# Norm factors folded into the weights, low weight parts on VectorE: a hybrid GLA and neighbourhood-attention layer

## The chip, the core and the metric

The kernel runs on one core of a Trainium2 chip. The metric is the device time of one launch in microseconds (us). The engines are named as in the profile: PE is TensorE (PEld its weight loads), DVE is VectorE, ACT is ScalarE, POOL is GpSimd, SP is the engine whose queue issues most DMAs.

## The reference

One encoder layer on 1024 tokens and 16 meta tokens of width 1024. The steps that matter here:

```
u = x * rsqrt(mean(x*x, -1) + eps) * norm_g          # pre-norm, norm_g has one factor per model column
z = u @ w_in                                          # one projection, its columns split into:
gq, gk, gv, r_f, r_b, g_gate, nq, nk, nv, n_gate = split(z)
# group A: gated linear attention, 4 heads, chunks of 64 tokens, a forward and a backward scan
o_gla = rmsnorm(scan_f(gq, gk, gv, decay(r_f)) + scan_b(...)) * silu(g_gate)
# group B: neighbourhood attention, 16 heads of 64, 8 x 16 window plus 16 meta keys
q, k = rmsnorm(nq) * q_norm_g, rmsnorm(nk) * k_norm_g
o_na = softmax(q k / 8 + rpb + meta_bias) v * silu(n_gate)
out = x + concat(o_gla, o_na) @ w_out
```

The factors norm_g stand on the contracted axis of the projection, so `(x*g) @ w` and `x @ (g*w)` are the same product; the factor 1/rms of a token is applied behind the projection, on its output.

## The kernel before, in words

**Products.** Every fp32 product is made of three TensorE passes over a high and a low part of each operand (`mm3`, L409 to L413): high x high (L411), high x low and low x high (L412, L413). A high part is a rounded copy, a low part what the rounding left. The token operand is kept whole in `uh` (high) and `ul` (low), eight blocks k of 128 model columns by 1024 tokens. The weights pass by in 150 pieces of up to 128x512, each loaded by an SP DMA into one of five `raw` buffers and split by `piece_split` (L240 to L261) into one of nine pairs of buffers, `wh` and `wl`. The split of piece j is followed on SP's queue by the load of piece j+5, into the raw buffer that it frees. A piece is split when a pair of buffers is free: `release` lets the next one go. Pieces of the attention pairs hold one block k ("pack" 1, 128x512, the first pair's 128x384); the last gate's pieces hold four blocks of 128 columns, the GLA pieces two of 256, the first GLA value pieces one of 288.

**Who splits before.** For most pieces of the first part of the kernel (tables `SPLIT_ACT` and `NA1_ACT`) ACT makes the high part (L254) and POOL the low part (L255); for the others DVE does both (L257, L258). From the second GLA head on (`gpool` set) ACT and DVE share it (L251, L252).

**Order of the work.** A planner with a clock of its own (`S`) emits the instructions: `S.defer(ns, f)` emits f when its clock has advanced by ns, and each engine then runs its own list in the order of emission. The first 60 us are laid out by hand (`START_AT`: at which product, counted over the first pair's tiles, a token tile is loaded, split, squared, its 1/rms made and spread).

**Stages.** (1) The start: the first pair's eight natural tiles (`pn_na`, 128 tokens by 384 columns, eight blocks k) are computed while tokens arrive. Tiles 0 and 1 are computed side by side (`first_pair`), their token parts made block by block (`u_part`, L341 to L346); tiles 2 to 7 by halves of a tile (`u_split`, L348 to L358), each half first multiplied by g on DVE (L354). `u_rstd` squares the token rows on ACT, into a PSUM bank (`junk`, L365), and POOL raises the mean to the power -1/2 (L210). To have 1/rms on all partitions, with tokens along the free axis (`rbc`, used by gates, L484), `u_diag` (L373) multiplies the identity by the column of 1/rms on DVE, and `u_spread` (L378) multiplies it by a block of ones on PE. Constants of the attention (`na_static`, L491 to L530) are copied into the key and query buffers K2 and Q2 on DVE. (2) Eight attention pairs p: the natural tiles of pair p+1 and then its gate (`pz_na`, transposed) are the bulk of PE's work, and the attention steps u of pair p (scores, softmax, transposes `pp` of the probabilities P, product with v) are laid between. In a step, P is normalised on DVE for its two halves a (reciprocal L813, multiplication L815), PE transposes it (L826), and the result is copied to SBUF, for a=0 on ACT (L830), for a=1 on DVE (L832). A pair's last natural tile gives its eight pairs of weight buffers back, so the splits of the next eight pieces stand around each pair's end, beside the attention step 7. `k_prep` opens a pair's attention: PE transposes the keys (`kt`, L693) after DVE has normalised them (`nat`, L557). (3) The GLA heads, (4) the output projection. Between (2) and (3) the decay weights are loaded (`wdst`), cut (`wd`, L1018 to L1022), and the first gates `gt` evacuated (L484).

Of the kernel before, what the change touches and what calls it, by code (L numbers as in the profile page):

```python
# [19 lines left out]
NKB = 8  # L20
# [30 lines left out]

START_AT = {'load': {2: 9, 3: 15, 4: 18, 5: 21, 6: 27, 7: 34}, 'split': {2: 15, 3: 19, 4: 25, 5: 28, 6: 41, 7: 48}, 'rows': {0: 10, 1: 12, 2: 18, 3: 21, 4: 23, 5: 29, 6: 45, 7: 53}, 'rstd': {0: 15, 1: 16, 2: 21, 3: 27, 4: 35, 5: 43, 6: 48, 7: 55}, 'evac': {0: 18, 1: 21, 2: 27, 3: 35, 4: 43, 5: 52, 6: 59}, 'diag': {0: 31, 1: 42, 2: 42, 3: 55, 4: 55}, 'spread': {0: 46, 1: 63, 2: 57, 3: 59}}
BANKS = {2: ("po", 1), 3: ("pp", 2), 4: ("pp", 2), 5: ("pd", 2), 6: ("pd", 2), 7: ("po", 1)}
PUMP_AT = 5
LD_NS = (842.0, 589.0, 1838.0)
LS_NS = (376.0, 9817.0, 2715.0, 3855.0)
# [4 lines left out]
GZ_DVE = (1, 1, 0, 1)  # L61

SPLIT_ACT = {'na': (1, 1, 1, 0), 'gz': (1, 0, 1, 0), 'gv': (1, 1, 1, 0), 'gg': (1, 0, 1, 0)}
NA1_ACT = (1, 0, 1, 0, 1, 1, 1, 1)
SILU_STEP = 1
# [71 lines left out]
def kernel(  # L137
# [105 lines left out]
    def piece_split(j):  # L243
        if j < len(pieces):
# [4 lines left out]
            r = raw.pop(j)  # L249
            if gpool[0] is not None:  # L250
                act.activation(wh[:, :n], r[:, :n], AF.Copy)  # L251
                dve.tensor_tensor(wl[:, :n], r[:, :n], f32(wh[:, :n]), OP.subtract)  # L252
            elif (NA1_ACT[j - 8] if 8 <= j < 16 else SPLIT_ACT[key[0]][j % 4]):
                act.activation(wh[:, :n], r[:, :n], AF.Copy)  # L254
                pool.tensor_tensor(wl[:, :n], r[:, :n], f32(wh[:, :n]), OP.subtract)  # L255
            else:
                dve.tensor_copy(wh[:, :n], r[:, :n])  # L257
                dve.tensor_tensor(wl[:, :n], r[:, :n], f32(wh[:, :n]), OP.subtract)  # L258
            for t in range(pack):
# [80 lines left out]
    def u_part(b, k):  # L340

        xk = xs[b][:, k * 128 : k * 128 + 128]
        ts = slice(b * 128, b * 128 + 128)
        g = gT[:, k : k + 1]
        act.activation(uh[:, k, ts], xk, AF.Copy, scale=g)
        dve.scalar_tensor_tensor(ul[:, k, ts], xk, g, f32(uh[:, k, ts]), OP.mult, OP.subtract)  # L346

    def u_split(b):  # L348

        ts = slice(b * 128, b * 128 + 128)  # L350
        x3 = xs[b].rearrange("p (k t) -> p k t", k=NKB)
        halves = (slice(0, 4), slice(4, 8))
        for ks in halves:
            dve.tensor_tensor(x3[:, ks], x3[:, ks], gT[:, ks, None].to_broadcast([128, 4, 128]), OP.mult)  # L354
        for ks in halves:
            act.activation(uh[:, ks, ts], x3[:, ks], AF.Copy)  # L356
        for ks in halves:
            dve.tensor_tensor(ul[:, ks, ts], x3[:, ks], f32(uh[:, ks, ts]), OP.subtract)  # L358

    def u_rstd(b):  # L360

        st = nap.tile([128, 2], F32, tag="ust", name=f"ust{b}", bufs=2)
        for i in range(2):
            junk = ps_tile("ps", f"junk{b}_{i}", 2)
            act.activation(junk, xr[b][:, 512 * i : 512 * i + 512], AF.Square, accum_out=st[:, i : i + 1])  # L365
        dve.tensor_tensor(st[:, 0:1], st[:, 0:1], st[:, 1:2], OP.add)
        rstd(rs[:, b : b + 1], st[:, 0:1], 1.0 / 1024, 1)

    dg = {}

    def u_diag(b):
        dg[b] = nap.tile([128, 128], F32, tag="dg", name=f"dg{b}", bufs=3)
        dve.tensor_scalar(dg[b], ident, rs[:, b : b + 1], None, OP.mult)  # L373

    def u_spread(b):

        ps = ps_tile("ps", f"rb{b}", 2)
        pe.matmul(ps[:, 0:128], ones, dg[b], start=True, stop=True)  # L378
        act.activation(rbc[:, b * 128 : b * 128 + 128], ps[:, 0:128], AF.Copy)
        S.adv(220)  # L380

    def u_meta():
# [16 lines left out]
        def parts():  # L399
            xv3 = xm[:, 0:128].rearrange("p (k t) -> p k t", k=NKB)  # L400
            dve.tensor_tensor(xv3, xv3, gT[:, :, None].to_broadcast([128, NKB, 16]), OP.mult)
            dve.tensor_tensor(xv3, xv3, r[:, None, :].to_broadcast([128, NKB, 16]), OP.mult)
# [89 lines left out]
    def na_static(part):  # L492
        if part == 0:
# [5 lines left out]
            def copies():  # L499
                dve.tensor_copy(K2[0][64:128, :, 0:128], sv[64:128])  # L500
                dve.tensor_copy(K2[1][0:64, :, 0:128], sv[0:64])

        elif part == 1:
# [31 lines left out]
    def dense_na(p):  # L535
# [65 lines left out]
        for b in range(8):  # L601
# [882 lines left out]
```

## Time and profile before

| what | value |
|---|---|
| device time, three runs | 1160.01, 1161.38, 1161.72 us; median 1161.38 us |
| profiled execution | 1161.92 us, of which 1159.1 us are the span of the trace |
| granted TensorE clock, mean | 0.997 of full speed |
| busy share of the span | PE 97%, PEld 85%, DVE 67%, ACT 46%, POOL 26% |

An engine's busy time is summed over the span; a page of the profile tells which groups of instructions it consists of, the view of waits tells what an engine stood still for, and the timeline gives single instructions with their start and duration in us. Three stages follow each other: the start until about 63 us, the attention pairs until about 629 us, GLA and output projection until the end.

### The profile page before, as it was taken

Reading aid. Unit: us, or ns where it says so; the run is one execution under the profiler, and the core shown is the slowest. Engines: PE = TensorE matmul, PEld = TensorE weight load, DVE = VectorE, ACT = ScalarE, POOL = GpSimd, SP = SyncE. Lnnn points to the kernel's source line nnn. Section 1 sums busy time; section 2 is a strip of 40 time slices with the busy share of each in tenths; the row PEclk is TensorE's granted clock in tenths of the full one; section 3 lists DMA queues with packets and bytes.
Section 4 is the critical chain, followed back from the end, with each engine's and each line's share of the span. In section 5 each row is a group of like instructions: output and inputs, shape, how many; then the busy total and the mean of one; then the engine's idle time right before and its main releaser. Section 6 shows DMA issues by size and latency. Waiting matters only on the chain.

```text
span 1159.1 us, 18919 instructions
## 1 busy us (share of the span) xinstructions
PE 1127.0 (97%) x6739; PEld 981.4 (85%) x6739; DVE 771.6 (67%) x1965; ACT 531.9 (46%) x1377; POOL 300.8 (26%) x415
## 2 busy tenths in 40 slices
PE   8899999999999999999999799999999999999998
PEld 7789898998989889898898689879978977788886
DVE  6966767677677776767664676675486578656352
ACT  6756565664656555465553342542343244212120
POOL 3753534335353433624323001101100100000000
PEclk9999999999999999999999899999999999999999
DMA  7720402103030120402025312512522365314132
GB/s 248 231 74 2 126 2 85 43 2 125 1 124 4 55 73 2 127 2 85 21 65 160 108 35 74 151 38 78 149 61 61 84 195 185 106 50 132 47 113 104
DMA packets 74277, 99.34 MB, mean 86 GB/s; under 512 B 6532, under 2 KB 45188, under 8 KB 74184
## 3 DMA queue, kind: packets, MB, share of 16 engines
q1 hardware_dynamic: 69960, 89.76, 25.3%
q0 software_dynamic: 4224, 8.39, 2.5%
q8 instruction: 53, 0.87, 0.3%
q14 instruction: 40, 0.33, 0.1%
HBM read 72.89 MB, written 21.04 MB: 81 GB/s over the span
## 4 chain that ended last, share of the span: by engine, by line
PE 81%; DVE 9%; issue 4%; ACT 2%; DMA 2%; POOL 1%; SPq 0%; POOLq 0%; DVEq 0%; ACTq 0%
PE pn_na L411 7%; PE pn_na L412 6%; PE pn_na L413 6%; PE pout L412 5%; PE pout L411 5%; PE pout L413 5%; PE po L845 4%; PE pp L826 3%; PE pz_na L411 2%; PE pz_na L413 2%; PE pz_na L412 2%; PE pz_gz L411 2%; PE pz_gz L412 2%; PE pz_gz L413 2%; PE pn_gv L411 2%
## 5 line engine op out<-in xcount | busy, mean ns | idle before, releaser
L411 PE MATMUL pn_na<-wh,uh 128*128 128x384 f32 x512 | 180.5, 352 | 1.1 <-ACT uh L356 0.6
L412 PE MATMUL pn_na<-wl,uh 128*128 128x384 f32 x512 | 174.1, 340 | 1.1 <-POOL wl L255 0.9
L413 PE MATMUL pn_na<-wh,ul 128*128 128x384 f32 x512 | 173.4, 339 | 0.2
L209 POOL TENSOR_SCALAR post<-post 128x1 f32<-128x1 f32 x32 | 7.4, 230 | 391.7 <-ACT on L1211 336.8
L411 PEld LDWEIGHTS pn_na<-wh,uh 128*128 128x128 f32 x512 | 96.2, 188 | 10.2 <-issue 8.1
L411 PE MATMUL pout<-wh,oh 128*128 128x512 f32 x256 | 102.9, 402 | 0.1
L412 PE MATMUL pout<-wl,oh 128*128 128x512 f32 x256 | 101.6, 397 | 0.0
L413 PE MATMUL pout<-wh,oh 128*128 128x512 f32 x256 | 100.8, 394 | 0.0
L412 PEld LDWEIGHTS pn_na<-wl,uh 128*128 128x128 f32 x512 | 96.3, 188 | 3.4 <-POOL wl L255 2.2
L413 PEld LDWEIGHTS pn_na<-wh,ul 128*128 128x128 f32 x512 | 96.1, 188 | 1.2 <-DVE ul L358 1.1
L255 POOL TENSOR_TENSOR wl<-raw,wh 128x512 fp32r<-128x512 f32 (+2 forms) x63 | 82.1, 1322 | 44.2 <-PE pn_gv L412 27.5
L1335 DVE TENSOR_TENSOR acc<-acc,pout 128x512 f32<-128x512 f32 x64 | 43.8, 685 | 66.0 <-PE pout L413 66.0
L798 ACT ACTIVATE P<-P,sm 128x384 f32<-128x384 f32 x96 | 58.5, 609 | 51.9 <-DVE sm L795 51.9
L411 PE MATMUL pn_gv<-wh,uh 128*128 128x256 f32 (+1 forms) x256 | 76.3, 298 | 0.0
L413 PE MATMUL pn_gv<-wh,ul 128*128 128x256 f32 (+1 forms) x256 | 73.0, 285 | 0.0
L412 PE MATMUL pn_gv<-wl,uh 128*128 128x256 f32 (+1 forms) x256 | 72.9, 285 | 0.0
L210 POOL TENSOR_TENSOR ss<-ss,epsm 128x4 f32<-128x4 f32 x64 | 70.3, 1099 | 5.3
L792 DVE CUSTOM_DVE_ANT_0 P<-s,wt 128x416 f32<-128x416 f32 (+1 forms) x128 | 69.6, 544 | 2.5 <-PE s L765 2.5
L815 DVE TENSOR_SCALAR P<-P,sm 128x384 f32<-128x384 f32 (+1 forms) x128 | 66.9, 522 | 4.5
L252 DVE TENSOR_TENSOR wl<-raw,wh 128x512 fp32r<-128x512 f32 x63 | 43.0, 689 | 28.6 <-ACT wh L251 27.0
L832 DVE COPY PT<-pp 128x384 f32<-128x384 f32 (+1 forms) x80 | 36.3, 470 | 37.0 <-PE pp L826 36.5
L411 PE MATMUL pz_gg<-uh,wh 128*128 128x512 f32 x128 | 53.1, 415 | 7.3 <-DVE gt L484 7.3
(361 smaller groups left out, 2962.8 us busy)
## 6 DMA issues: line engine op xcount, KB each, us to landing
raw<-in_w_na_dram SPq DMA_DIRECT2D x56, 256.0 KB, 2.8
v_scr<-gvst SPq DMA_DIRECT2D x64, 128.0 KB, 2.3
raw<-in_w_o_dram SPq DMA_DIRECT2D x32, 256.0 KB, 3.1
oin<-o_scr SPq DMA_DIRECT2D x32, 256.0 KB, 3.0
v<-v_scr POOLq DMA_DIRECT2D x4, 1536.0 KB, 8.3
VM<-vnat SPq DMA_DIRECT2D x8, 512.0 KB, 4.7
o_scr<-ng SPq DMA_DIRECT2D x8, 512.0 KB, 3.5
raw<-in_w_gz_dram SPq DMA_DIRECT2D x16, 256.0 KB, 2.8
```

Of the source, the lines that this page charges most:

```text
L210: pool.tensor_tensor(dst, dst, epsm[: dst.shape[0], :eng_n], OP.pow)
L252: dve.tensor_tensor(wl[:, :n], r[:, :n], f32(wh[:, :n]), OP.subtract)
L255: pool.tensor_tensor(wl[:, :n], r[:, :n], f32(wh[:, :n]), OP.subtract)
L411: pe.matmul(ps, ah, bh, start=start, stop=False)
L412: pe.matmul(ps, ah, bl, start=False, stop=False)
L413: pe.matmul(ps, al, bh, start=False, stop=stop)
L792: dve.tensor_tensor_reduce(P[:, :n], ps[:, :n], wt[2 * p + a][:, off : off + n], 1.0, -3.0e38, OP.add, OP.max, mx)
L798: act.activation(loc, loc, AF.Exp, bias=mx, accum_out=sm[:, a : a + 1])
L815: dve.tensor_scalar(loc, loc, r, None, OP.mult)
L832: dve.tensor_copy(t[:w, e0:e1], pp[:w, e0:e1])
L845: pe.matmul(po[0][64 * a : 64 * a + 64, u4 * 128 : u4 * 128 + 128], V[:, 64 * a : 64 * a + 64], PT[a][:w, c * 128 : c * 128 + 128], start= ...
L1335: dve.tensor_tensor(a, a, ps, OP.add)
```

## The change

The factors g go into the weights: for every piece but those of the output projection, ACT writes the high part as a copy scaled by the g of its block, and DVE writes the low part in one instruction, raw times g minus high (`scalar_tensor_tensor`); a piece that packs two or four blocks needs two or four such pairs of instructions. POOL makes no low parts any more. The token parts are plain copies and differences. The spread of 1/rms takes the column of 1/rms, repeated along the free axis, as one operand of the matmul and the identity as the other, so `u_diag` and its places in the order go. The squares are written over the token rows in SBUF, not into a PSUM bank. The constant copies of K2 and Q2 go from DVE to ACT.

```diff
-START_AT = {..., 'diag': {0: 31, 1: 42, 2: 42, 3: 55, 4: 55}, 'spread': {0: 46, 1: 63, 2: 57, 3: 59}}
+START_AT = {..., 'spread': {0: 46, 1: 63, 2: 57, 3: 59}}
-LD_NS = (842.0, 589.0, 1838.0)
-SPLIT_ACT = {'na': (1, 1, 1, 0), 'gz': (1, 0, 1, 0), 'gv': (1, 1, 1, 0), 'gg': (1, 0, 1, 0)}
-NA1_ACT = (1, 0, 1, 0, 1, 1, 1, 1)
@@ piece_split
-            if gpool[0] is not None:
+            if key[0] == "o":
                 act.activation(wh[:, :n], r[:, :n], AF.Copy)
                 dve.tensor_tensor(wl[:, :n], r[:, :n], f32(wh[:, :n]), OP.subtract)
-            elif (NA1_ACT[j - 8] if 8 <= j < 16 else SPLIT_ACT[key[0]][j % 4]):
-                act.activation(wh[:, :n], r[:, :n], AF.Copy)
-                pool.tensor_tensor(wl[:, :n], r[:, :n], f32(wh[:, :n]), OP.subtract)
-            else:
-                dve.tensor_copy(wh[:, :n], r[:, :n])
-                dve.tensor_tensor(wl[:, :n], r[:, :n], f32(wh[:, :n]), OP.subtract)
+            for t in range(pack if key[0] != "o" else 0):
+                ts = slice(t * (n // pack), (t + 1) * (n // pack))
+                g = gT[:, pack * i + t : pack * i + t + 1]
+                act.activation(wh[:, ts], r[:, ts], AF.Copy, scale=g)
+                dve.scalar_tensor_tensor(wl[:, ts], r[:, ts], g, f32(wh[:, ts]), OP.mult, OP.subtract)
@@ u_part
-        g = gT[:, k : k + 1]
-        act.activation(uh[:, k, ts], xk, AF.Copy, scale=g)
-        dve.scalar_tensor_tensor(ul[:, k, ts], xk, g, f32(uh[:, k, ts]), OP.mult, OP.subtract)
+        act.activation(uh[:, k, ts], xk, AF.Copy)
+        dve.tensor_tensor(ul[:, k, ts], xk, f32(uh[:, k, ts]), OP.subtract)
@@ u_split
-        for ks in halves:
-            dve.tensor_tensor(x3[:, ks], x3[:, ks], gT[:, ks, None].to_broadcast([128, 4, 128]), OP.mult)
@@ u_rstd
-            junk = ps_tile("ps", f"junk{b}_{i}", 2)
-            act.activation(junk, xr[b][:, 512 * i : 512 * i + 512], AF.Square, accum_out=st[:, i : i + 1])
+            half = xr[b][:, 512 * i : 512 * i + 512]
+            act.activation(half, half, AF.Square, accum_out=st[:, i : i + 1])
@@ u_diag, u_spread
-        dve.tensor_scalar(dg[b], ident, rs[:, b : b + 1], None, OP.mult)
-        pe.matmul(ps[:, 0:128], ones, dg[b], start=True, stop=True)
+        pe.matmul(ps[:, 0:128], rs[:, b : b + 1].to_broadcast([128, 128]), ident, start=True, stop=True)
@@ u_meta
-            dve.tensor_tensor(xv3, xv3, gT[:, :, None].to_broadcast([128, NKB, 16]), OP.mult)
@@ na_static
-                dve.tensor_copy(K2[0][64:128, :, 0:128], sv[64:128])
-                dve.tensor_copy(K2[1][0:64, :, 0:128], sv[0:64])
+                act.activation(K2[0][64:128, :, 0:128], sv[64:128], AF.Copy)
+                act.activation(K2[1][0:64, :, 0:128], sv[0:64], AF.Copy)
...
@@ dense_na, end of the first pair
-                    if i:
-                        S.defer(LD_NS[i - 1], lambda i=i: u_diag(4 + i))
                     S.defer(LS_NS[i], lambda i=i: u_spread(4 + i))
```

The list of PE keeps its instructions and their order, and so does SP's. The lists of DVE, ACT and POOL change. (A row of either kernel has the line numbers of that kernel.) The first place is DVE at the end of the first pair, before:

```order
L552 TENSOR_REDUCE ss0_6_685<-sq0_6_684 128x4
L257 CAST wh11_699<-raw11_543 128x512
L258 TENSOR_TENSOR wl11_700<-raw11_543,wh11_699 128x512
L500 CAST K2_0_93<-xv_100 64x8x128
L501 CAST K2_1_94<-xv_100 64x8x128
L552 TENSOR_REDUCE ss0_7_735<-sq0_7_734 128x4
L373 TENSOR_SCALAR dg6_751<-ident_76,rs_80 128x128
L373 TENSOR_SCALAR dg5_759<-ident_76,rs_80 128x128
L557 TENSOR_TENSOR nat0_6_687<-nat0_6_687,ss0_6_685 128x256
L373 TENSOR_SCALAR dg7_774<-ident_76,rs_80 128x128
L557 TENSOR_TENSOR nat0_7_737<-nat0_7_737,ss0_7_735 128x256
L688 TENSOR_SCALAR kmr_102<-kmt0_799,gk_t_82 128x16
```

and now, from the square sums of tile 6 (`ss0_6`) to the scaled meta keys `kmr`:

```order
L537 TENSOR_REDUCE ss0_6_646<-sq0_6_645 128x4
L253 SCALAR_TENSOR_TENSOR wl11_661<-raw11_515,gT_79,wh11_660 128x512
L253 SCALAR_TENSOR_TENSOR wl12_675<-raw12_615,gT_79,wh12_674 128x512
L253 SCALAR_TENSOR_TENSOR wl13_690<-raw13_453,gT_79,wh13_689 128x512
L537 TENSOR_REDUCE ss0_7_696<-sq0_7_695 128x4
L253 SCALAR_TENSOR_TENSOR wl14_713<-raw14_625,gT_79,wh14_712 128x512
L542 TENSOR_TENSOR nat0_6_648<-nat0_6_648,ss0_6_646 128x256
L253 SCALAR_TENSOR_TENSOR wl15_726<-raw15_640,gT_79,wh15_725 128x512
L253 SCALAR_TENSOR_TENSOR wl16_738<-raw16_664,gT_79,wh16_737 128x512
L542 TENSOR_TENSOR nat0_7_698<-nat0_7_698,ss0_7_696 128x256
L671 TENSOR_SCALAR kmr_102<-kmt0_754,gk_t_82 128x16
```

The low parts of pieces 12 to 16, which POOL made before, now stand on DVE ahead of the normalised keys of tiles 6 and 7 (`nat0_6`, `nat0_7`); the identity products `dg` are gone. The second place is DVE at the end of the second pair, beside the attention step 7 of pair 0 (`sm07`, `P070`, `P071`; `PT061` is the transposed P of step 6), before:

```order
L832 COPY PT061_1483<-pp061_1479 128x384
...
L813 RECIPROCAL sm07_1485<-sm07_1485 128x1
L815 TENSOR_SCALAR P070_1489<-P070_1489,sm07_1485 128x272
L257 CAST wh19_1517<-raw19_757 128x512
L258 TENSOR_TENSOR wl19_1518<-raw19_757,wh19_1517 128x512
L813 RECIPROCAL sm07_1485<-sm07_1485 128x1
L815 TENSOR_SCALAR P071_1496<-P071_1496,sm07_1485 128x272
L557 TENSOR_TENSOR nat1_6_1457<-nat1_6_1457,ss1_6_1455 128x256
L832 COPY PT071_1567<-pp071_1563 128x256
```

and now:

```order
L253 SCALAR_TENSOR_TENSOR wl17_1423<-raw17_678,gT_79,wh17_1422 128x512
L815 COPY PT061_1438<-pp061_1434 128x384
...
L253 SCALAR_TENSOR_TENSOR wl18_1459<-raw18_693,gT_79,wh18_1458 128x512
L796 RECIPROCAL sm07_1440<-sm07_1440 128x1
L798 TENSOR_SCALAR P070_1444<-P070_1444,sm07_1440 128x272
L253 SCALAR_TENSOR_TENSOR wl19_1473<-raw19_716,gT_79,wh19_1472 128x512
L796 RECIPROCAL sm07_1440<-sm07_1440 128x1
L798 TENSOR_SCALAR P071_1451<-P071_1451,sm07_1440 128x272
L253 SCALAR_TENSOR_TENSOR wl20_1490<-raw20_729,gT_79,wh20_1489 128x512
```

The low part of piece 17 now stands ahead of the copy of `PT061`, those of pieces 18 and 19 ahead of the two reciprocals, and those of 20 to 22 ahead of the copies of step 7, where before one piece was split on DVE (a CAST and a subtraction) between the two normalisations.

## Rows read from the trace of the kernel before

**Rows 1.** Busy time by stretch (columns: window, us, PE, PEld, DVE, ACT, POOL, PEclk, DMA, GB/s).

```profile
0.00:10.00 10.00, 8.25 (x35) 7.01 (x36) 4.21 (x6) 4.02 (x8) 3.62 (x10) 1.00 0.73 229
10.00:63.00 53.00, 45.20 (x242) 39.06 (x242) 44.03 (x97) 36.60 (x101) 33.92 (x45) 1.00 0.71 228
30.00:40.00 10.00, 9.03 (x51) 8.39 (x50) 9.37 (x24) 9.29 (x27) 6.69 (x10) 1.00 0.94 328
63.00:629.00 566.00, 562.03 (x3708) 502.16 (x3708) 399.39 (x1186) 323.09 (x917) 225.93 (x283) 1.00 0.18 56
642.00:646.00 4.00, 3.55 (x8) 2.81 (x9) 0.99 (x2) 0.00 (x0) 0.00 (x0) 0.50 0.30 96
```

**Rows 2.** What PE waited for (us in total, times, longest).

```profile
PE pz_gg L411 <- DVE gt L484: 7.3, 2, 6.3
PE pp L826 <- DVE P L815: 4.0, 6, 0.7
PE pkt L1191 <- DVE mt L1141: 3.4, 4, 1.8
PE rb L378 <- DVE dg L373: 3.0, 2, 2.2
...
PE pm_na L469 <- DVE um L404: 1.1, 1, 1.1
...
PE kt L693 <- DVE nat L557: 0.9, 1, 0.9
PE rb L378 <- ACT junk L365: 0.9, 1, 0.9
```

**Rows 3.** Groups by line (busy us, mean ns of one; then idle before, by releaser).

```profile
L254 ACT ACTIVATE wh<-raw 128x512 fp32r<-128x512 f32 x51 | 30.7, 625 | 2.7 <-DMA raw<-in_w_na_dram 1.4 <-DMA raw<-in_w_gv_dram 0.9 <-DMA raw<-in_w_gz_dram 0.4
L345 ACT ACTIVATE uh<-x,gT 128x128 fp32r<-128x128 f32 x16 | 5.5, 389 | 4.1 <-DMA x<-in_xt_dram 2.6 <-DMA gT<-in_normg_dram 1.5
L403 ACT ACTIVATE um<-xm 128x128 fp32r<-128x128 f32 x1 | 0.3, 309 | 0.8 <-DVE xm L402 0.8
L715 DVE SCALAR_TENSOR_TENSOR K<-kt,gk_t,K 64x512 fp32r<-64x512 f32 x32 | 24.0, 749 | 0.9
L971 DVE SCALAR_TENSOR_TENSOR gvst<-pn_gv,rs,gvst 128x256 fp32r<-128x256 f32 x32 | 15.4, 482 | 16.8 <-ACT gvst L970 16.5
L252 DVE TENSOR_TENSOR wl<-raw,wh 128x512 fp32r<-128x512 f32 x63 | 43.0, 689 | 28.6 <-ACT wh L251 27.0 <-PE pk L1160 1.0 <-PE pa L1241 0.2
```

**Rows 4.** Single instructions of the start, POOL, DVE and PE (start, us, instruction [idle before]).

```profile
11.85 3.05 POOL L255 TENSOR_TENSOR wl<-raw,wh 128x384 fp32r<-128x384 f32 x3 [3.46 <-ACT wh L254]
...
15.23 0.35 DVE L257 CAST wh<-raw 128x384 fp32r<-128x384 f32 x1
...
28.94 0.44 PE L411 MATMUL pn_na<-wh,uh 128*128 128x384 f32 x1 [0.34 <-ACT uh L356]
...
62.83 0.33 PE L693 MATMUL kt<-ident,nat 128*128 128x128 f32 x1 [0.91 <-DVE nat L557]
```

**Rows 5.** A pair's end on ACT, DVE, POOL and PE, and normalisations elsewhere.

```profile
119.05 0.64 ACT L254 ACTIVATE wh<-raw 128x512 fp32r<-128x512 f32 x1
...
121.38 0.18 ACT L802 ACTIVATION_READ_ACCUMULATOR P<-P,sm 128x1 f32 x1
...
119.26 0.56 DVE L832 COPY PT<-pp 128x384 f32<-128x384 f32 x1 [0.26 <-PE pp L826]
...
124.10 1.18 DVE L815 TENSOR_SCALAR P<-P,sm 128x272 f32<-128x272 f32 x1
...
608.14 0.36 DVE L815 TENSOR_SCALAR P<-P,sm 128x272 f32<-128x272 f32 x1
...
119.37 1.01 POOL L210 TENSOR_TENSOR ss<-ss,epsm 128x4 f32<-128x4 f32 x1
...
125.43 0.52 PE L826 MATMUL pp<-ident,P 128*128 128x128 f32 x3 [0.66 <-DVE P L815]
...
537.78 0.82 PE L826 MATMUL pp<-ident,P 128*128 128x128 f32 x6
```

More of the change, by code (lines that the diff above doesn't have):

```diff
@@ L50 @@
 GSIG1_NS = 3111.0
-START_AT = {'load': {2: 9, 3: 15, 4: 18, 5: 21, 6: 27, 7: 34}, 'split': {2: 15, 3: 19, 4: 25, 5: 28, 6: 41, 7: 48}, 'rows': {0: 10, 1: 12, 2: 18, 3: 21, 4: 23, 5: 29, 6: 45, 7: 53}, 'rstd': {0: 15, 1: 16, 2: 21, 3: 27, 4: 35, 5: 43, 6: 48, 7: 55}, 'evac': {0: 18, 1: 21, 2: 27, 3: 35, 4: 43, 5: 52, 6: 59}, 'diag': {0: 31, 1: 42, 2: 42, 3: 55, 4: 55}, 'spread': {0: 46, 1: 63, 2: 57, 3: 59}}
+START_AT = {'load': {2: 9, 3: 15, 4: 18, 5: 21, 6: 27, 7: 34}, 'split': {2: 15, 3: 19, 4: 25, 5: 28, 6: 41, 7: 48}, 'rows': {0: 10, 1: 12, 2: 18, 3: 21, 4: 23, 5: 29, 6: 45, 7: 53}, 'rstd': {0: 15, 1: 16, 2: 21, 3: 27, 4: 35, 5: 43, 6: 48, 7: 55}, 'evac': {0: 18, 1: 21, 2: 27, 3: 35, 4: 43, 5: 52, 6: 59}, 'spread': {0: 46, 1: 63, 2: 57, 3: 59}}
 BANKS = {2: ("po", 1), 3: ("pp", 2), 4: ("pp", 2), 5: ("pd", 2), 6: ("pd", 2), 7: ("po", 1)}
 PUMP_AT = 5
-LD_NS = (842.0, 589.0, 1838.0)
 LS_NS = (376.0, 9817.0, 2715.0, 3855.0)
@@ L363, in u_rstd @@
         for i in range(2):
-            junk = ps_tile("ps", f"junk{b}_{i}", 2)
-            act.activation(junk, xr[b][:, 512 * i : 512 * i + 512], AF.Square, accum_out=st[:, i : i + 1])
+            half = xr[b][:, 512 * i : 512 * i + 512]
+            act.activation(half, half, AF.Square, accum_out=st[:, i : i + 1])
         dve.tensor_tensor(st[:, 0:1], st[:, 0:1], st[:, 1:2], OP.add)
         rstd(rs[:, b : b + 1], st[:, 0:1], 1.0 / 1024, 1)
-    dg = {}
-    def u_diag(b):
-        dg[b] = nap.tile([128, 128], F32, tag="dg", name=f"dg{b}", bufs=3)
-        dve.tensor_scalar(dg[b], ident, rs[:, b : b + 1], None, OP.mult)
     def u_spread(b):
         ps = ps_tile("ps", f"rb{b}", 2)
-        pe.matmul(ps[:, 0:128], ones, dg[b], start=True, stop=True)
+        pe.matmul(ps[:, 0:128], rs[:, b : b + 1].to_broadcast([128, 128]), ident, start=True, stop=True)
         act.activation(rbc[:, b * 128 : b * 128 + 128], ps[:, 0:128], AF.Copy)
@@ L511, in copies @@
                     es = slice(256 * e, 256 * e + 256)
-                    dve.tensor_copy(Q2[0][e][64:128], ho[64:128, es])
-                    dve.tensor_copy(Q2[1][e][0:64], ho[0:64, es])
+                    act.activation(Q2[0][e][64:128], ho[64:128, es], AF.Copy)
+                    act.activation(Q2[1][e][0:64], ho[0:64, es], AF.Copy)
         else:
@@ L588, in at @@
                 ("load", x_load), ("split", u_split), ("rows", x_rows), ("rstd", u_rstd),
-                ("evac", lambda t: tile_evac(banks.pop(t), t)), ("diag", u_diag), ("spread", u_spread),
+                ("evac", lambda t: tile_evac(banks.pop(t), t)), ("spread", u_spread),
             ):
```

## The prediction

> **What bounds the kernel.** I read the busy time by stretch first. From 63 to 629 us, the attention pairs, PE is busy in 562.03 of 566 us [rows 1]: whatever the change takes from POOL or gives to DVE, at most 3.97 us can be won there. In the first 63 us PE is idle in 9.55 us (1.75 and 7.80), while DMA and ACT are near their limit in one stretch of it (94% and 93% from 30 to 40 us). Then I read what PE waits for [rows 2]. At the start these are mostly waits for DVE and ACT that the change touches: 3.0 us for the identity products, 0.9 for the `junk` banks, 1.1 for the meta parts, 0.9 for the normalised keys. In the pairs it is one kind alone: 4.0 us in six waits of the transposes `pp` for the normalised P. Behind them there is one long wait, 6.3 us for the first `gt` of the last gates, and in GLA 3.4 us for `mt`. So the change is worth what it does to these waits and to the chains that end in them; PE's own instructions stay the same in kind, shape and order.
>
> **Prices.** A high part now is a scaled ACT copy. The unscaled one takes 625 ns; scaling shows as 389 against 309 ns on 128x128 (the scaled token copy and the unscaled meta copy), +80 ns [rows 3]: I take 0.71 us for 128x512. The low part, a `scalar_tensor_tensor` with a pointer scalar, isn't there in this shape. Its bounds are 689 ns (the plain subtraction of the same shape) and 749 ns (the same operation on 64x512, which reads PSUM); I take 0.75. POOL's low part on the start's 128x384 took 3.05/3 = 1.02 us each [rows 4]; a 128x256 half costs DVE 482 ns [rows 3], so a piece of two halves costs 0.96 at most instead of 0.69, and as instructions on one engine overlap a little I count +0.2.
>
> **The start, -6.5 us.** POOL's three low parts ran one behind the other from 11.85 to 14.90, and a CAST on DVE only began at 15.23, behind token parts that DVE did slowly beside POOL [rows 4]. With ACT 0.6 and DVE 0.6 per piece of 384 columns, walking both engines' new lists from the landing of each raw piece, I get the end of the first pair 1.9 us earlier. Without the multiplication by g ahead of a half tile's copy, tile 4, which begins at 28.94, starts at about 26.0, where its tokens' landing binds. From there each wait of rows 2 up to the keys was followed in turn: the `junk` wait of 0.9 goes since the squares need no bank, the two waits for identity products (3.0) go with them, and the meta wait shrinks; together with the 2.9 won by tile 4 and less than full gain in the DMA-bound stretch, the tiles end about 6 to 7.5 us earlier. What is late next is the first `kt`: key tile 7 now stands behind the low parts of pieces 15 and 16 on DVE, and their high parts stand on ACT behind the two mask copies of 1024 columns, about 1.06 us each by an estimate from ACT's 309 ns on 128 and 625 ns on 512 columns. That gives `kt` at about 56.2 instead of 62.83 [rows 4]: -6.6, of which I keep -6.5. Bounds: PE has 7.80 us idle from 10 to 63 us [rows 1], so the gain cannot pass -7.8; if DMA and ACT, at over 90% in the middle stretch, hold the tiles where they are, only the waits behind it go and `kt` keeps growing, -2.5.
>
> **The ends of seven pairs, +4.0 us.** Before, the high part of the next pair's first piece was on ACT at 119.05, and DVE could copy PT at 119.26 [rows 5]. Now the low part of that piece stands ahead of this copy on DVE: high part until 119.76, low part until 120.5, and the copy starts at about 120.47, +1.21 us. The scores of step 7 stand behind it on DVE, so the exponentials, read at 121.38 to 121.56, are read at 122.77. The second piece's low part stands ahead of the first normalisation, and its high part on ACT behind the exponentials: high 122.68 to 123.39, low 123.43 to 124.18, P of a=0 124.30 to 124.66, the third piece's low part until 125.33, P of a=1 125.45 to 125.81. PE's transpose, which before started at 125.43 after a wait of 0.66, starts at 125.86: +0.43. It isn't +1.21 since DVE is freed from POOL: the normalisation took 1.18 us at 124.10, beside POOL's low parts, and 0.36 at 608.14, with none beside it [rows 5]. Behind the transposes PE has its own work, and every such delay counts, as nothing else is left for PE there. Six times 0.43 is 2.6. At the seventh end, before the last gate, PE did not wait (transposes at 537.78); its first piece is of four parts, four ACT and four DVE instructions, so the copy of PT is later by about 1.38 and the transpose of a=1 comes at 539.57 instead of 538.2: +1.4. Together +4.0. Bounds: -4 (all six waits vanish, if DVE is quicker than I reckon) and +8.5 (seven times the full 1.21).
>
> At one place a rule speaks against this. In the rows, POOL's power (L210) runs from 119.37 to 120.38 [rows 5], just when the new low part would start. The Trainium skill, "SBUF — State Buffer", section "Who interferes with whom", says that a VectorE instruction with two inputs in SBUF contends with a GpSimd instruction that reads SBUF, and that the later one is fully blocked; by that rule the low part waits until 120.38, and the case is a rival below. The trace agrees for POOL's low parts (the 1.18 above); for the power it has no such row at this place.
>
> **GLA, +1.5 us.** The last POOL low part goes, so the decay weights are asked for about 0.65 us earlier and the wait of 6.3 us shrinks by as much; PE's clock stands at 0.50, the lower of its two levels (1.2 GHz), from 642 to 646 us after that wait [rows 1], and I leave that as it is. Against it, each piece of two parts costs DVE 0.2 more, and PE waits for DVE's `gt` and `mt` in each head [rows 2]: four pieces ahead of each wait make 0.6 for three heads and 0.3 for the last, +2.1. Bounds: 0 (the pieces lie in DVE's free time) and +3 (the 6.3 doesn't shrink and a head pays 0.8). In the output projection nothing changes.
>
> **Sum.** -6.5 + 4.0 + 1.5 = -1.0 us, against the profiled execution 1161.92 us (span 1159.1) gives 1160.9. That execution was 0.5 above the median of the runs, so against the median I forecast 1160.4.
>
> **Rivals.** *The pairs' waits go as well.* POOL makes no low parts, so DVE's normalisations take 0.36 instead of 1.18; if the high parts reach ACT earlier, or DVE overlaps its instructions more than I count, the transposes do not wait. For it: the waits at the pair ends are beside POOL's work. Against it: the low parts are ahead of the softmax in DVE's list. -6.5 at the start, -2 of the possible -4 at the pairs, +1.5: -7, that is 1154.5. *The pairs pay in full.* The low part ahead of PT's copy delays the whole of step 7 by 1.21 and the relief does not show, because a=1's normalisation was slow for another reason: 7 x 1.21 = 8.5, with -6.5 and +1.5 gives +3.5; 1165. It decides as soon as a pair's end costs over 0.85 us, for then seven outweigh start and GLA by over 1. For it: PE has no idle time between, so nothing absorbs a delay. *POOL's powers block DVE.* The low part held until 120.38 instead of 119.80 adds 0.58 at each of seven ends, +4.1: 1164.5. The rule of the Trainium skill named above is its ground. *The start doesn't gain*, the change not doing what it removes work for: DMA keeps the tiles where they are, -2.5 + 4.0 + 1.5 = +3, 1164.4; it needs the same bound for 20 us, and only one stretch of 10 us shows 94%.
>
> **Chances.** The forecast 0.45, its own range 1158.5 to 1162.5; pairs' waits gone 0.30; pairs in full 0.10; POOL's powers 0.08; no gain at the start 0.07. A measurement of this kernel tells about 0.2%, 2.3 us, from no change: faster is below 1159.1, slower above 1163.7. Faster holds the second case and a quarter of the first (0.40), slower most of the last three (0.22), the rest is the same (0.38). The range, 1153.5 to 1165.5, takes in both neighbours.
>
> **What would show it.** Right: the first `kt` near 56.2; the matmuls after the start with no wait for `rb`; `pp` waiting in seven places for about 1.1 us, 1.4 at the last gate; normalisations back at 0.36; the wait for `gt` at 5.6; `mt` waits up by about 0.6. Wrong: no `pp` waits at all (second case), low parts of 1.3 us beside POOL's powers (fourth), or `kt` after 60 (fifth). A stage that isn't in the sum, the output projection or the steps within a pair, coming out otherwise would mean that the change moves something that I have not seen.

## The result, and the profile after

| kernel | median, us | runs |
|---|---|---|
| before | 1161.33 | 20 |
| changed | 1163.06 | 20 |

The ratio is 1.0018 with a 95% interval of 1.0010 to 1.0027: about 2 us slower, where 1 us faster was forecast. The two profiled executions have spans of 1159.07 and 1160.45 us. PE runs the same 6739 matmuls in the same order in both, so the start of each one can be set against its counterpart. Times are in us; a place keeps its name when it moves. That gives the whole difference by place:

| place | start before | start after | after minus before |
|---|---|---|---|
| tile 4, first product | 28.94 | 26.38 | -2.56 |
| last key transpose of the first pair | 62.83 | 57.20 | -5.63 |
| transposes of P (a=0), end of the second pair | 124.28 | 119.19 | -5.09 |
| the same, sixth of these ends | 468.85 | 466.32 | -2.53 |
| transposes of a=1, seventh end | 538.11 | 537.06 | -1.05 |
| transposes of a=1 in the last attention | 589.73 | 590.18 | +0.45 |
| first product after the wait for `gt` | 642.45 | 642.66 | +0.21 |
| end of the span | 1159.07 | 1160.45 | +1.38 |

What PE waits for in the changed kernel (us in total, times, longest), to be set against [rows 2]:

```profile
PE pp L809 <- DVE P L798: 8.3, 15, 1.3
PE pz_gg L396 <- DVE gt L469: 7.2, 2, 6.1
PE pkt L1174 <- DVE mt L1124: 3.7, 4, 1.8
PE kt L676 <- DVE nat L542: 1.6, 2, 1.3
```

The waits for identity products and for `junk` are gone; in the place of the longer one for identity products PE now waits 1.0 us for ACT's copy of an earlier spread (`rbc`, 0.99 at 52.15). The wait for `gt` has shrunk by 0.2 us only, and the waits for the normalised P have doubled, from 4.0 to 8.3 us. The busy time by stretch (columns as in [rows 1]) says the same in another way:

```profile
10.00:63.00 53.00, 48.76 (x268) 44.11 (x269) 32.64 (x86) 44.30 (x117) 21.85 (x38) 1.00 0.76 251
63.00:629.00 566.00, 557.66 (x3680) 496.94 (x3678) 390.56 (x1224) 338.25 (x948) 162.08 (x230) 1.00 0.17 54
```

PE's idle time falls from 7.80 to 4.24 us between 10 and 63 us and rises from 3.97 to 8.34 us from 63 to 629 us. DVE is busy for less time in the pairs than before (390.56 against 399.39 us) and PE still waits longer for it: the order on DVE has become worse, its load has not. The prices were as reckoned (busy us, mean ns):

```profile
L253 DVE SCALAR_TENSOR_TENSOR wl<-raw,gT,wh 128x512 fp32r<-128x512 f32 x56 | 41.3, 743 | 18.0 <-ACT wh L252 18.0
...
L252 ACT ACTIVATE wh<-raw,gT 128x512 fp32r<-128x512 f32 x56 | 38.2, 714 | 2.9 <-DMA raw<-in_w_na_dram 2.8
L253 DVE SCALAR_TENSOR_TENSOR wl<-raw,gT,wh 128x256 fp32r<-128x256 f32 x88 | 38.0, 481 | 25.1 <-ACT wh L252 24.5 <-PE pu L398 0.3
```

DVE stands idle for 18.0 us ahead of low parts, because the high part isn't there yet. That idle time is the story of the end of a pair. Single instructions of DVE, POOL and PE there, in the changed kernel, against [rows 5]:

```profile
114.21 0.75 DVE L253 SCALAR_TENSOR_TENSOR wl<-raw,gT,wh 128x512 fp32r<-128x512 f32 x1 [0.81 <-ACT wh L252]
114.88 0.55 DVE L815 COPY PT<-pp 128x384 f32<-128x384 f32 x1
...
117.81 0.75 DVE L253 SCALAR_TENSOR_TENSOR wl<-raw,gT,wh 128x512 fp32r<-128x512 f32 x1 [1.30 <-ACT wh L252]
...
118.68 0.36 DVE L798 TENSOR_SCALAR P<-P,sm 128x272 f32<-128x272 f32 x1
118.95 0.75 DVE L253 SCALAR_TENSOR_TENSOR wl<-raw,gT,wh 128x512 fp32r<-128x512 f32 x1
...
119.81 0.36 DVE L798 TENSOR_SCALAR P<-P,sm 128x272 f32<-128x272 f32 x1
...
113.76 1.01 POOL L206 TENSOR_TENSOR ss<-ss,epsm 128x4 f32<-128x4 f32 x1
...
119.19 0.52 PE L809 MATMUL pp<-ident,P 128*128 128x128 f32 x3 [0.36 <-DVE P L798]
120.31 0.52 PE L809 MATMUL pp<-ident,P 128*128 128x128 f32 x3 [0.61 <-DVE P L798]
```

A low part waits for ACT (0.81), the copy of P for the low part, the scores for the copy, the exponentials for the scores, and the second low part again for ACT, behind the exponentials (1.30). PE waits 0.97 us (0.36 and 0.61) where it waited 0.66. POOL's power (113.76 to 114.77) ran beside the first low part, which took 0.75 all the same, as it did at the five ends that follow.

### The profile page after: what moved, and what is told of

It reads as the page before. It is cut to its first block, busy times and chain, and to the rows that moved or that the text cites. A ratio compares the mean times of both kernels' runs of the same rounds, so it can differ in the third digit from the quotient of the medians.

```text
span 1160.4 us, 19040 instructions
## 1 busy us (share of the span) xinstructions
PE 1127.2 (97%) x6739; PEld 981.7 (85%) x6739; DVE 756.5 (65%) x2027; ACT 564.8 (49%) x1457; POOL 220.4 (19%) x352
## 4 chain that ended last, share of the span: by engine, by line
PE 81%; DVE 8%; ACT 5%; DMA 3%; issue 2%; SPq 0%; POOL 0%; ACTq 0%; DVEq 0%; POOLq 0%
PE pn_na L396 7%; PE pn_na L397 6%; PE pn_na L398 6%; PE pout L396 5%; PE pout L397 5%; PE pout L398 5%; PE po L828 4%; PE pp L809 3%; PE pn_gv L396 3%; PE pn_gv L398 2%; PE pn_gv L397 2%; PE pz_na L396 2%; PE pz_na L398 2%; PE pz_na L397 2%; DVE wl L253 2%; PE pz_gz L396 2%
## 5 line engine op out<-in xcount | busy, mean ns | idle before, releaser
L253 DVE SCALAR_TENSOR_TENSOR wl<-raw,gT,wh 128x256 fp32r<-128x256 f32 (+4 forms) x168 | 91.4, 576 | 49.9 <-ACT wh L252 49.2
L252 ACT ACTIVATE wh<-raw,gT 128x256 fp32r<-128x256 f32 (+4 forms) x168 | 88.3, 572 | 24.9 <-PE pz_gz L397 12.3
L206 POOL TENSOR_TENSOR ss<-ss,epsm 128x4 f32<-128x4 f32 x64 | 66.6, 1041 | 5.3
L809 PE MATMUL pp<-ident,P 128*128 128x128 f32 (+1 forms) x384 | 54.1, 274 | 8.3 <-DVE P L798 8.3
L798 DVE TENSOR_SCALAR P<-P,sm 128x384 f32<-128x384 f32 (+1 forms) x128 | 59.0, 461 | 4.5
L205 POOL TENSOR_SCALAR ss<-ss 128x4 f32<-128x4 f32 x64 | 19.3, 301 | 221.2 <-DVE ss L537 160.3
```

The source lines that it names most:

```text
L206: pool.tensor_tensor(dst, dst, epsm[: dst.shape[0], :eng_n], OP.pow)
L252: act.activation(wh[:, ts], r[:, ts], AF.Copy, scale=g)
L253: dve.scalar_tensor_tensor(wl[:, ts], r[:, ts], g, f32(wh[:, ts]), OP.mult, OP.subtract)
L798: dve.tensor_scalar(loc, loc, r, None, OP.mult)
L809: pe.transpose(pp[:w, c * 128 : c * 128 + 128], Ps[a][0][:, c0 : c0 + w], ident)
```

## The experiments

The numbers below are ratios to the kernel before on the same chip, with the 95% interval; PE's places are set against the first trace of the kernel before, as in the table.

**Low parts behind the softmax.** This is called the reordered kernel below. The edit holds the low part, and the load that follows it; `soft` is set from a step's scores to its second normalisation, and the numbers 17 to 65 in steps of eight are the first pieces of the pairs' ends:

```diff
+            if gs and (soft[0] or (17 <= j <= 65 and (j - 9) % 8 == 0)):
+                lows.append(low)      # issued at the end of norm(1)
...
+            else:
+                low()
```

> The changed kernel, with the low parts that fall between a step's scores and its second normalisation, and the first one of each pair's end, issued on DVE behind that normalisation; their raw buffers are asked for again as much later. Same instructions, another order. Theory A (DVE's order: a low part that waits for its high part on ACT stands at the head of DVE's queue before the softmax): the 8.3 us that PE waits for the normalised P go almost wholly, the first matmul of the gate that follows the seventh end comes at about -5.5 us against the kernel before instead of -1.05, the wait of 1.3 us near 590 goes, and the time is about 7 us below the changed kernel's (5 to 8.3), near 1156. Rival B (DVE's and ACT's added work itself, 0.75 and 0.72 us per piece): the waits move from the normalisations to the low parts or to the next steps, and no more than 2 us are won.

Measured: 0.9953 (0.9938 to 0.9968), 1152.39 us. PE's waits, without any line for the normalised P:

```profile
PE pz_gg L413 <- DVE gt L492: 7.4, 2, 6.3
PE pkt L1203 <- DVE mt L1153: 3.6, 4, 1.8
PE kt L699 <- DVE nat L565: 1.6, 2, 1.3
```

The same instructions, in another order, and all 8.3 us are gone, those near 590 us with them. At the seventh end (a=1) PE now starts 10.45 us earlier than before, not 1.05: more than expected, since the six waits of the kernel before go too. By the two ratios the time is 7.5 us below the changed kernel's, though the two ran on different chips. Theory A holds.

**Everything but the split.** The changed kernel with the split of the kernel before:

```diff
-            if key[0] == "o":
+            if gpool[0] is not None:
...
+            elif (NA1_ACT[j - 8] if 8 <= j < 16 else SPLIT_ACT[key[0]][j % 4]):
...
+                pool.tensor_tensor(wl[:, :n], r[:, :n], f32(wh[:, :n]), OP.subtract)
```

> The changed kernel with the split of the kernel before (tables, POOL making most low parts) and norm_g left out of the computation altogether, so that only the other edits stay: no multiplication of tokens by g, no identity products, squares in place, constants copied on ACT. Theory A: the pairs' ends are as before the change, six waits of 0.66 for the normalised P and none near 590, so what the start wins is kept to the end; the start wins about 3.5 us (the first pair's 1.8 that came with the low parts stay lost), and the time is about 1158. Rival B (the start's gain comes from the low parts on DVE): the first keys no more than 1.5 us earlier than before, about 1160. Rival C (the loss at the pairs' ends comes from the start's edits, for instance the shifted order of the constants): the ends still lose 0.5 each, and the time is 1161 or more.

Measured: 0.9969 (0.9958 to 0.9979).

```profile
PE pp L812 <- DVE P L801: 4.6, 7, 0.7
PE pkt L1177 <- DVE mt L1127: 3.4, 4, 1.8
PE kt L679 <- DVE nat L545: 1.8, 1, 1.8
```

The last key transpose comes 5.80 us earlier than before, as early as in the changed kernel. So the start's gain comes from the other edits (token parts, spread, squares, constants) and not from the low parts on DVE; the 1.1 us that these win in the first pair (-2.00 in the changed kernel against -0.93 here, at the product that stood at 19.55) are lost again where tile 4 waits for its tokens (26.57 here, 26.38 there). The six ends stay as they were, the seventh loses 0.82 (PE waits 0.66 there too), and nothing happens near 590. B and C fall; A holds for the ends but one and was too low for the start. This kernel leaves norm_g out.

**Constants on DVE.**

```diff
-                act.activation(K2[0][64:128, :, 0:128], sv[64:128], AF.Copy)
...
+                dve.tensor_copy(K2[0][64:128, :, 0:128], sv[64:128])
...
```

> The changed kernel with the four constant copies for K2 and Q2 on DVE again. Theory A (the last keys wait for low parts 15 and 16, whose high parts stand behind two mask copies of 1.06 us on ACT): the last key transpose comes 0.8 us earlier than in the changed kernel (56.4 instead of 57.2), and the time falls by as much. Rival B (DVE is as late with 1.4 us of copies in front of the same low parts): no difference within 0.3 us. Rival C: the gate's first products wait for a high part or for the spread of 1/rms on ACT, not for DVE, and the gate's matmuls come 1 us earlier while the last keys do not.

Measured: 1.0060 (1.0039 to 1.0080). All three theories are wrong: it got worse. The last key waits longer, and behind that wait the granted clock is at 0.50, the lower of the two levels (1.2 GHz), for 3.4 us:

```profile
57.92 0.33 PE L676 MATMUL kt<-ident,nat 128*128 128x128 f32 x1 [2.42 <-DVE nat L542]
```

```profile
59.10:62.50 3.40, 3.40 (x11) 2.62 (x10) 1.16 (x4) 1.93 (x4) 0.00 (x0) 0.50 0.27 108
```

Over that stretch PE falls back by another 1.5 us (-4.91 to -3.39). DVE, not ACT, is what these keys wait for. They do not explain the whole ratio: in this trace the wait for `gt` is 8.4 instead of 6.1 us as well, because the second decay weight landed late (DVE stood idle 1.8 us for it), which nothing here ties to the constants.

**Packed pieces in one instruction each.**

```diff
-            if key[0] == "o":
+            if pack > 1 or key[0] == "o":
...
-            for t in range(pack if key[0] != "o" else 0):
+            for t in range(1 if pack == 1 and key[0] != "o" else 0):
```

> The changed kernel with the pieces that pack two or four blocks split in one instruction each on ACT and DVE, which leaves norm_g out of the last gate's and the GLA's weights. Theory A (pieces cut in parts cost DVE 0.2 and ACT 0.25 us more each, and PE waits for DVE in each head): the loss of 0.93 us beyond a normal pair's end at the seventh end and the 0.86 us lost from 592 us to the end go, together -1.8 us, the wait near 590 shrinks by less than 0.5. Rival B (GLA's loss is not from the parts): only the seventh end gains, -0.9.

Measured: 1.0036 (1.0022 to 1.0049), on the chip of the three runs above. The time settles nothing, as its trace has low-clock stretches at 673 and 761 us that the changed kernel's has not. By place: the seventh end costs 0.94 instead of 1.48, the place near 590 waits 1.12 instead of 1.32, and the steps of 0.48, 0.43 and 0.30 at 696, 759 and 860 us in the GLA heads are gone. By place A holds; by time it isn't shown.

**Both kernels once more, on one chip.**

> The kernel before, unchanged, for its own spread of times and clocks and a second trace. Theory A: the places of PE's work up to the 6.3 us wait near 642 us are those of the first trace within 0.3 us, the six waits of 0.66 are there, and what differs from one execution to another is how many stretches of about 4 us run at the lower clock (each 1.5 to 2 us). Rival B: other waits differ too, so that a comparison of two single traces carries an error of more than 1 us before 642 us.

> The changed kernel, unchanged, beside the kernel before on the same chip. Theory A: 0.1 to 0.3% slower as in the first comparison, with a start of -5.6, seven ends of together +4.6, +1.5 near 590 and +0.9 behind it. Rival B (the loss is larger where the kernel before runs faster, as the packed-piece variant at +0.36% suggests): 0.35% or more slower, by more stretches of lower clock or by waits that its trace names.

Measured: the changed kernel 1.0010 (0.9999 to 1.0021), so on this chip the loss is not clear of noise. Its places lose as before (0.51 to 0.57 per end at six ends, 1.50 near 590), and its start wins less (-4.88 at the last key). The kernel before: 0.9994 (0.9979 to 1.0008). But in its second trace PE does not wait at the six ends at all. DVE, POOL and PE there:

```profile
121.88 0.69 DVE L258 TENSOR_TENSOR wl<-raw,wh 128x512 fp32r<-128x512 f32 x1
...
122.68 1.20 DVE L815 TENSOR_SCALAR P<-P,sm 128x272 f32<-128x272 f32 x1
...
121.88 6.01 POOL L255 TENSOR_TENSOR wl<-raw,wh 128x512 fp32r<-128x512 f32 x4 [0.53 <-ACT wh L254]
...
124.00 0.82 PE L826 MATMUL pp<-ident,P 128*128 128x128 f32 x6
```

and in the first trace:

```profile
122.18 1.82 DVE L258 TENSOR_TENSOR wl<-raw,wh 128x512 fp32r<-128x512 f32 x1
...
122.16 5.70 POOL L255 TENSOR_TENSOR wl<-raw,wh 128x512 fp32r<-128x512 f32 x4 [0.51 <-ACT wh L254]
```

Where POOL began 20 ns ahead, DVE's low part took 1.82 us; where both began at 121.88 it took 0.69, and POOL's first low part 1.84 instead of 1.28. All six ends of either trace are like this, and the seventh of the first trace shows the other case within one execution: both begin at 535.67, DVE's takes 0.69, and PE does not wait. So the waits on which a term of the prediction rests come and go from one execution to another (PE gains 3.2 us from the last key to 470 us in the second trace). Rival B for the kernel before holds, and theory A for the changed one, its start apart.

**That tie taken away.** In the kernel before, DVE's low parts behind the normalisation:

```diff
+            elif soft[0]:
                 dve.tensor_copy(wh[:, :n], r[:, :n])
+                lows.append(lambda: dve.tensor_tensor(wl[:, :n], r[:, :n], f32(wh[:, :n]), OP.subtract))
...
```

> The kernel before, with the low parts that DVE makes between a step's scores and its second normalisation issued behind that normalisation; POOL's stay. Theory A (the six waits of 0.66 come from a tie: DVE's low part and POOL's, 20 ns apart, and the one that starts second is held): with no low part of DVE in that place the transposes of P wait at no pair's end in any execution, the time falls by 2 to 4 us against the kernel before (less where most of its executions win the tie), and the times spread less. Rival B: DVE's normalisation itself is held beside POOL (1.18 us), and the six waits stay at 0.4 or more.

> The changed kernel with late low parts once more, on the chip of the run above, to set the change against the kernel before with both in the better order. Theory A (in that order the change keeps its start, -5.5, and loses about 1 us in GLA): 3.5 to 5 us faster than the reordered kernel before. Rival B (POOL's relief was worth nothing and the reorder alone is the gain): the two within 1.5 us.

Measured: 0.9966 (0.9952 to 0.9980) and 0.9935 (0.9914 to 0.9956); 1156.33 and 1152.06 us. DVE and PE in the former:

```profile
121.87 1.37 DVE L838 TENSOR_SCALAR P<-P,sm 128x272 f32<-128x272 f32 x1
...
123.91 0.82 PE L852 MATMUL pp<-ident,P 128*128 128x128 f32 x6
```

No transpose waits at a pair's end, though the normalisation still took 1.37 us beside POOL: the low part ahead of it was the cause. With both kernels in the better order, the change is worth 4.3 us by the medians, and the slowest run of the changed one (1154.72) is faster than the fastest of the other (1154.88). Theory A holds in both. What the new split alone is worth in that order was not run.

**Which low part.** Only the first one of each end moved, first behind the normalisation, then only behind the scores. The edit against the reordered kernel:

```diff
-            if gs and (soft[0] or (17 <= j <= 65 and (j - 9) % 8 == 0)):
+            flush_lows()      # in the second run only
+            if gs and 17 <= j <= 65 and (j - 9) % 8 == 0:
```

> The changed kernel with only the first low part of each pair's end, from the second pair on, moved behind the normalisation; those ahead of the reciprocals stay. Theory A (the first low part, which moves the scores by 1.2 us, is the whole loss at six ends, for with it gone everything behind comes 1.2 us earlier and PE waited 0.36 and 0.61): no waits of the transposes at six ends, at the seventh below 0.5, and the wait of 1.3 near 590 stays as it is; 4.5 to 6 us below the changed kernel. Rival B (the low parts between exponentials and reciprocals are what is late): waits of 0.3 to 1 stay at each end, and less than 3 us are won.

> As the run with the first low part moved, but moved only behind the scores of step 7, ahead of the next low part, so that the loads of raw pieces keep their order on SP's queue (there the load for the moved piece went behind two others, and PE waited up to 2 us for it at each pair's end). Theory A (the first low part ahead of the copy of P is the whole loss at six ends): DVE stands idle for the exponentials anyway, so the six ends have no waits of the transposes, the seventh at most 0.5, the one of 1.3 us near 590 stays, no new wait of the gate's products; 5 to 6 us below the changed kernel (about 0.997 of it or less). Rival B (low parts two and three ahead of the reciprocals bind): waits of 0.3 us or more stay at each end.

The first run: 1.0094 (1.0065 to 1.0124), 9.5 us slower than the kernel before, where a time 4.5 to 6 us below the changed kernel's was expected. The waits for the normalised P at the ends went, and a new wait came, as the held low part also held the load of a later raw piece, which then went behind two others on SP's queue. PE waits so seven times, 11.3 us in all, in the profiled execution (1182.13 us, the slowest of five, at a mean granted clock of 0.983). ACT and PE there:

```profile
125.03 0.72 ACT L254 ACTIVATE wh<-raw,gT 128x512 fp32r<-128x512 f32 x1 [3.42 <-DMA raw<-in_w_na_dram]
...
126.79 0.50 PE L413 MATMUL pz_na<-uh,wh 128*128 128x512 f32 x1 [1.79 <-ACT vnat L558]
```

The second run, with the loads in order: 0.9961 (0.9946 to 0.9976). DVE and PE:

```profile
116.10 0.75 DVE L258 SCALAR_TENSOR_TENSOR wl<-raw,gT,wh 128x512 fp32r<-128x512 f32 x1
117.47 0.75 DVE L258 SCALAR_TENSOR_TENSOR wl<-raw,gT,wh 128x512 fp32r<-128x512 f32 x1 [0.62 <-ACT wh L254]
...
119.54 0.95 PE L837 MATMUL pp<-ident,P 128*128 128x128 f32 x6
```

The first low part now runs while DVE would wait for the exponentials, and no transpose waits at the six ends, though the other two low parts still stand ahead of the reciprocals. One instruction too early in DVE's list was nearly the whole loss there: each of these ends now gains 0.7 us against the kernel before, where the reordered kernel gains 0.8 and the changed one lost 0.5. The seventh loses 0.3. The wait of 1.3 us near 590 stayed, as expected, and by the two ratios the time is 6.6 us below the changed kernel's. Theory A holds.

**Identity products again.**

```diff
...
-        pe.matmul(ps[:, 0:128], rs[:, b : b + 1].to_broadcast([128, 128]), ident, start=True, stop=True)
+        pe.matmul(ps[:, 0:128], ones, dg[b], start=True, stop=True)
```

> The changed kernel with the identity products on DVE again (eight of 128x128) and ones as the stationary operand. Theory A (these waits were a part of the start's gain by themselves: 0.8 and 2.2 us): the first gate's spreads wait for DVE again, by 1 to 2.5 us in all, and the time rises by that. Rival B (the identity products were late only because DVE was held beside POOL): with no low parts on POOL they are in time, waits under 0.4 us, and the time stays.

Measured: 1.0027 (1.0014 to 1.0041), against 1.0010 for the changed kernel on the same chip.

```profile
PE rb L371 <- DVE dg L366: 3.1, 2, 2.7
```

The waits are back in full with no low part on POOL: A by the waits, so the spread without identity products removes waits of its own. By time it is not settled, as the two intervals overlap; the medians differ by 2.6 us. Part of this is the clock: from 55.5 to 62.3 us, behind the longer wait, the granted clock in this trace is 0.50, the lower level.

**The last keys first.** On top of the reordered kernel:

```diff
-            if gs and (soft[0] or (17 <= j <= 65 and (j - 9) % 8 == 0)):
+            if gs and (soft[0] or (17 <= j <= 65 and (j - 9) % 8 == 0) or 14 <= j <= 16):
...
+                if p == 0 and b == 7:      # behind the last key tile
+                    flush_lows()
```

> The reordered kernel (low parts behind the softmax), and in addition the low parts of pieces 14 to 16 behind the keys of tile 7. Theory A (the last key of the first pair waits for low parts 14 to 16 on DVE, not for its square sums): the last key transpose comes at 55.7 instead of 57.3, its wait falls from 1.3 to 0.3 us or less, and the time falls by 1.2 to 1.6 against the reordered kernel. Rival B: the gate's products then wait for low parts 14 and 15, and nothing is won.

Measured: 0.9915 (0.9898 to 0.9932), 1152.44 us. DVE and PE:

```profile
55.64 0.42 DVE L565 TENSOR_TENSOR nat<-nat,ss 128x256 f32<-128x256 f32 x1 [1.17 <-POOL ss L206]
...
56.12 0.33 PE L701 MATMUL kt<-ident,nat 128*128 128x128 f32 x1 [0.29 <-DVE nat L565]
...
58.26 0.44 PE L733 MATMUL qt<-ident,nat 128*128 128x128 f32 x2 [0.40 <-DVE kmr L696]
```

The last key transpose comes at 56.12 and its wait falls from 1.3 to 0.3, as A has it, but half of that comes back behind the low parts, where the transposes of the queries (`qt`) wait until DVE has scaled the meta keys (`kmr`): -6.14 instead of -5.50 at 64 us. Its time does not differ from the reordered kernel's 1152.39 and 1152.06 on other chips; whether 0.6 us are won stays open. Both beat the kernel before and the changed one.

## Why the prediction was wrong

The mechanisms named were there, but their sum left one place out, and it decides the sign: -1.0 forecast and +1.50 at that place is +0.5. The other three terms missed by +0.87, +0.58 and -0.57, which makes the +1.38 of the two traces.

- **Start.** Forecast -6.5, measured -5.63. The first pair (-2.0 for -1.9) and tile 4 (26.38 for 26.0) came as worked out. Of the 3.0 us of waits for identity products 1.0 came back as the wait for `rbc`; even so PE is 6.47 us early at that place. The last key came at 57.20, not 56.2: low part 14 waits 0.67 for ACT ahead of key tile 6, and low parts 15 and 16 stand ahead of key tile 7. DVE there:

```profile
54.39 0.75 DVE L253 SCALAR_TENSOR_TENSOR wl<-raw,gT,wh 128x512 fp32r<-128x512 f32 x1 [0.67 <-ACT wh L252]
55.06 0.42 DVE L542 TENSOR_TENSOR nat<-nat,ss 128x256 f32<-128x256 f32 x1
55.40 1.41 DVE L253 SCALAR_TENSOR_TENSOR wl<-raw,gT,wh 128x512 fp32r<-128x512 f32 x2
56.73 0.42 DVE L542 TENSOR_TENSOR nat<-nat,ss 128x256 f32<-128x256 f32 x1
```

  With these low parts behind the keys, in the last run above, the transpose came at 56.12.

- **The ends of seven pairs.** Forecast +4.0, measured +4.58: 0.49 to 0.53 at six (0.43 forecast), 1.5 at the seventh (1.4). The chain written out instruction by instruction held to 0.1 us. One of its reasons did not hold: the relief was put down to the normalisation of 1.18 us, which is as slow in the second trace (1.20), where PE does not wait. The low part of 1.82 us ahead of it made the wait.
- **The step that failed** is that this term counted seven places, as if pieces were split beside an attention step only at the ends of pairs. The last attention runs beside the first GLA head, whose pieces are split in the middle of its steps. DVE there in the kernel before, with no low part among its normalisations:

```profile
585.94 0.16 DVE L812 TENSOR_TENSOR sm<-sm 128x1 f32<-128x1 f32 x1 [0.51 <-ACT P L799]
...
587.71 0.73 DVE L815 TENSOR_SCALAR P<-P,sm 128x384 f32<-128x384 f32 x1
```

  ACT, DVE and PE in the changed kernel:

```profile
584.88 0.19 ACT L782 ACTIVATION_READ_ACCUMULATOR P<-P,sm 128x1 f32 x1
...
585.91 0.19 ACT L782 ACTIVATION_READ_ACCUMULATOR P<-P,sm 128x1 f32 x1
586.00 1.32 ACT L252 ACTIVATE wh<-raw,gT 128x288 fp32r<-128x288 f32 x3
...
586.56 0.52 DVE L253 SCALAR_TENSOR_TENSOR wl<-raw,gT,wh 128x288 fp32r<-128x288 f32 x1 [1.97 <-ACT wh L252]
...
588.38 0.87 DVE L253 SCALAR_TENSOR_TENSOR wl<-raw,gT,wh 128x256 fp32r<-128x256 f32 x2
...
589.55 0.48 DVE L798 TENSOR_SCALAR P<-P,sm 128x384 f32<-128x384 f32 x1
...
590.18 0.52 PE L809 MATMUL pp<-ident,P 128*128 128x128 f32 x3 [1.32 <-DVE P L798]
```

  Four exponentials stand ahead of the high part on ACT (the last is read at 585.91), so DVE idles for 1.97 us with the low part at the head of its queue, while the sums of the first half a, ready from 585.07 on, stand behind it. Two low parts of the next piece (0.87 us) then stand ahead of the second half's sums. That is +1.50, not in the sum. The second run with only the first low parts moved keeps this wait and the reordered kernel loses it, which shows that the order on DVE is its cause. The prediction had named it as a sign of something not seen if a step within a pair came out otherwise.
- **GLA.** Forecast +1.5, measured +0.93 (from +0.45 to +1.38): the pieces in parts cost 0.3 to 0.5 in three heads (0.6 forecast each), the last head won 0.4 where it was to lose 0.3, and the wait for `gt` shrank by 0.2 instead of 0.65. DVE could begin to cut the decay weights at 635.72 instead of 635.03, 0.69 us later, while PE's work ahead of the wait was 0.44 us later: they landed no earlier relative to PE.
- **Rivals.** "The pairs pay in full" had the right sign and the wrong size. The measured 1163.06 us is near the times of three rivals (1164.4 to 1165), but by luck: a pair's end cost 0.5 and not 1.21, the start gained 5.63 and not 2.5, and POOL's powers did not hold DVE. The first low part took 0.75 us beside such a power at each of the six ends, so the rule of the Trainium skill's "SBUF — State Buffer" ("Who interferes with whom") does not hold for that instruction here, while POOL's low parts do hold DVE (1.82 against 0.69 us). The prediction's row for that agreement, the normalisation of 1.18 us, is of an instruction that reads one tensor and one scalar per partition, not two tensors; the low part of 1.82 us is the row that bears on the rule. That the pairs' waits go as well did not come with this order, but came with the reordered one.
- **The base.** The six waits of 0.66 stood in the trace that was read, but not in every execution; one trace could not tell that. They are worth about 3 us, more than the 1 us that was forecast.

## What to carry to other kernels

When work moves to an engine, lay out that engine's new list at every place where the moved instructions land, the odd ones too, and ask of each what it waits for and what stands ready behind it: an engine with a third of its time free still delays others through one early instruction. An instruction that waits for another engine belongs behind work that is ready, and its followers (here a load that shares its buffer) must keep their own order. A wait that rests on which of two instructions starts 20 ns ahead is no base for a sum.

## What had not been expected of the hardware

Stretches of about 3.4 us at the lower clock (0.50, 1.2 GHz) come in some executions in places where others have none. In the second trace of the kernel before (columns as in [rows 1]):

```profile
59.00:62.40 3.40, 3.40 (x14) 2.74 (x13) 2.33 (x5) 0.65 (x2) 3.23 (x5) 0.50 0.48 146
...
670.00:673.40 3.40, 3.40 (x11) 2.53 (x9) 0.54 (x3) 1.28 (x3) 0.00 (x0) 0.50 0.00 0
```

The first trace has neither: from 55 to 59 us PE is busy for 1.80 us in both, and only in the second does the clock fall at 59.0. What decides it no run here shows. Of the fourteen traces seven have such a stretch about the last keys and seven have one about 30 us behind the wait for `gt`. The one at 59 us cost nothing at the last key, where PE had waited 0.91 us for DVE in the first trace; in the one at 670 us PE loses 1.4 us against the first trace (-4.17 to -2.77 from the start to the end of it). The wait for `gt` differs from trace to trace too, 5.6 and 6.3 us in the two traces of the reordered kernel, and 8.2 to 8.5 in three traces in which the second decay weight landed late. Of the 20 runs of the changed kernel, those with a mean clock of 0.993 or 0.994 took 1163.2 to 1166.1 us and those with 0.997 took 1161.1 to 1162.6 us, so a loss of 2 us can't be read from a few runs.
